# A two-layer sequence mixer: root-mean-square norms by a power on GpSimd, and a rebuilt first stage

## The chip, the core and the metric

The kernel runs on one core of a Trainium2 chip. The metric is the device time of one execution in microseconds (us). TensorE (PE) multiplies matrices, VectorE (DVE) and ScalarE (ACT) do elementwise work, GpSimd (POOL) does a few transfers, a broadcast over partitions and some elementwise work, and SyncE's queue (SP) issues nearly all transfers from memory.

## The reference, cut to what matters

```
def _rmsnorm(x, g):
    y = x * lax.rsqrt(jnp.mean(x * x, axis=-1, keepdims=True) + EPS)
    return y * g

shift, scale, gate = split(silu(c) @ mod_w[layer] + mod_b[layer], 3)
h = _rmsnorm(x, norm_g) * (1 + scale) + shift
# layer 0: u, g = split(h @ rg_w_in); conv over 4 steps; gated linear recurrence; out projection
# layer 1: k, v from their own norm and modulation of x; q, g = split(h @ att_w_in); causal attention; out projection
x = x + gate * y            # after each layer
return _rmsnorm(x, final_norm_g)
```

x is 256 x 1024 in float32, and every weight is 1024 wide. Four norms are taken, two of them of the same x after layer 0.

## The kernel before, in words

x is held as two tiles of 128 rows (s = 0, 1) by 1024. All weights come in blocks of 512 KB from one packed array, in the order of the table `ORDER`, into a ring of 11 buffers (`NRAW`). A product in near float32 is made of three passes: each operand is split into a rounded high part (suffix `_hi`) and the rest (`_lo`), and `mm3` or `gemm_m` adds hi*hi, hi*lo and lo*hi in PSUM.

The program isn't issued as it is written. Each call is recorded by `_Recorder` (line 409 of the profile is the recorder's call, so most rows carry L409; L169 is `Plan.copy` and its kin, which may go to ACT or DVE). `Plan.order` then simulates the engines with fixed costs and writes an order of instructions for each engine; 80 random changes of the urgencies are tried, and the best order is kept. Every engine then takes its instructions strictly in that order. `warm` adds matmuls on a tile of ones that nothing reads ("fillers"); the planner puts them where it sees TensorE idle.

The stages, in the order of time:

1. **First stage.** c, mod_b, norm_g and x are loaded. `rms` squares each row half on ACT with a running sum, takes the root on ACT, and on DVE a reciprocal and one Newton step; `norm_T` scales x by it, and TensorE transposes it (`tp_a`) into xnT. The modulation of the first two groups of 128 columns comes from `mod_one` (32 small matmuls `gvm0s`, then `mc_m0s`), later ones from `mod_pair` or `mod_sum`. `mod_apply` makes h0, split in hi and lo, and `u_rows(k)` (24 matmuls each) and `pair_T` (`ga`) multiply it by the input weights.
2. **Gates and recurrence.** Matmuls `pa` and `px` of the convolved u, then a long row of ACT functions and DVE scans, and the out projection `r_wo`.
3. **Norm b.** x1 = x + gate * y by `resid`; the gate row is gathered by four DMAs on GpSimd's queue (`row_g`) and spread over all partitions by GpSimd's `partition_broadcast` (`gate_g`). Then `rms`, `norm_T`, and the v, k, g and q products, one long run of matmuls.
4. **Attention**, head by head, mixed with the first half of the out projection `r_wp`.
5. **The end.** `fin` runs after each piece of `r_wp`: x2 = x1 + gate * y, `rms` of x2 in two or three parts, times `final_norm_g` (`fgB`), times the root's inverse, and the transfer out. For s = 0 the product with fgB is GpSimd's (two instructions, `ot`); for s = 1 it is DVE's, in place in x2.

The lines that matter most, of `rms`:

```
A.activation(sq, row, AF.Square, accum_out=ss)
A.activation(v, ss, AF.Sqrt, bias=bias, scale=1.0 / D)
V.reciprocal(y, v)
V.scalar_tensor_tensor(t, y, nv, y, ALU.mult, ALU.mult)
V.scalar_tensor_tensor(y, t, 1.5, y, ALU.add, ALU.mult)
```

Of the kernel before, what the change touches and what calls it, by code (L numbers as in the profile page):

```python
# [18 lines left out]
P = 128  # L19
# [7 lines left out]
NRAW = 11  # L27
NSPL = 4
NWARM = 16
NWARM2 = 4  # L30
SUM0 = 3
# [4 lines left out]
    s0 wu0 s1 wu1 wga0 m01 wu2 wu3 m02 wga1 wu4 wu5 m03 wga2 wu6 wu7 wga3 wgc0 gax0 gax2 gax3 g0-0  # L36
    gax1 wgc1 g0-1 wo0 mk0 mk1 wo1 mk4 mk2 mk3 mk5 wv0 mk7 mk6 wv1 wv2 wv3 m10 wka0 wka1 wv4 wv5
    wka2 m12 wv6 m11 wv7 m13 m15 wka3 m14 wkb0 m16 m17 wkb1 wgb0 wgb1 wqa0 wgb2 wgb3 wqa1 wgb4 wgb5
    wqa2 wgb6 wgb7 wqa3 wqb0 wqb1 g1-0 wp0 wp1 g1-1
"""  # L40

# [6 lines left out]
def blocks():  # L48
# [14 lines left out]
    for b in ORDER.split():  # L63
        nm, i = b[:-1], int(b[-1])
        if nm == "s":
            for x, c0 in (("h", 0), ("c", D)):
                want(f"m0{x}0_{i}", (KT, P), ("mod_w", 0, 0, D, c0 + i * P, P))
        elif nm == "m0" and i >= SUM0:
# [31 lines left out]


BLOCKS = blocks()


# [15 lines left out]
class Plan:  # L120
# [165 lines left out]

    def _forward(self, urge):
# [12 lines left out]
        while len(seq) < n:  # L300
# [52 lines left out]
        return max(fin), start, eng, sorted(range(n), key=lambda i: (start[i], i))  # L353

# [7 lines left out]
    def order(self):  # L362
# [15 lines left out]
        rnd = random.Random(self.SEED)  # L378
        for _ in range(self.ROUNDS):
            part, far = rnd.choice((0.003, 0.01, 0.05, 0.3)), rnd.choice((500, 3000, 10000))  # L380
            other = [u + rnd.gauss(0, far) if rnd.random() < part else u for u in urge]
            got = self._forward(other)
            if got[0] <= best[0]:
                best, urge = got, other
# [8 lines left out]
    ROUNDS, SEED = 80, 4  # L393
# [35 lines left out]
def kernel(ctx: ExitStack, tc: tile.TileContext, x, c, mod_b, norm_g, rg_conv_w, rg_conv_b,  # L429
                       rg_b_a, rg_b_x, rg_lambda, kv_norm_g, kv_mod_b, final_norm_g, pack, out):  # L430
# [16 lines left out]
    x, c, out = x[0], c[0], out[0]  # L447
# [13 lines left out]
    def split_into(raw, hi, lo):  # L461
        plan.copy(hi, raw)
        V.tensor_sub(lo, raw, hi.bitcast(F32))


    def wsplit(name):
        while len(halves) <= windex[name]:
# [5 lines left out]
            split_into(t, hi, lo)  # L473
# [86 lines left out]
    th = const.tile([KT, P], F32, name="cth")  # L560
    A.activation(th, c8, AF.Tanh, scale=0.5)
    V.scalar_tensor_tensor(c8, th, 1.0, c8, ALU.add, ALU.mult)
    pt = bank("pt_c")
    PE.transpose(pt[:, 0:KT], c8, ident[0:KT, 0:KT])
    csB = const.tile([P, KT, 32], F32, name="csB")
    V.tensor_scalar(csB, pt[:, 0:KT].unsqueeze(2).broadcast_to([P, KT, 32]), 0.5, None, ALU.mult)
    csT = const.tile([P, KT], F32, name="csT")
    V.tensor_scalar(csT, pt[:, 0:KT], 0.5, None, ALU.mult)
# [3 lines left out]


    def rms(nm, parts, early=None):
        bias, nbias = eps, neps
        for i, row in enumerate(parts):
            w = row.shape[-1]
            sq = tmp.tile([P, w], F32, tag="xn" if w > 512 else "tg", name=f"sq_{nm}{i}")
            if early is not None and i == 0:
                A.activation(sq[0:early.shape[0], 0:1], early, AF.Sqrt, scale=0.0)  # L580
            ss = small.tile([P, 1], F32, tag="ss", name=f"ss_{nm}{i}", bufs=4)
            A.activation(sq, row, AF.Square, accum_out=ss)
            if i < len(parts) - 1:
                b = small.tile([P, 2], F32, tag="rb", name=f"rb_{nm}{i}", bufs=4)
                V.tensor_scalar(b[:, 0:1], ss, 1.0 / D, bias, ALU.mult, ALU.add)
                V.tensor_scalar(b[:, 1:2], ss, -0.5 / D, nbias, ALU.mult, ALU.add)
                bias, nbias = b[:, 0:1], b[:, 1:2]
# [11 lines left out]
    def norm_T(row, rstd, xnT, s, nm):  # L599
        xn = tmp.tile([P, D], F32, tag="xn", name="xn_" + nm, bufs=2)  # L600
        plan.scale(xn, row, rstd)
        for q in range(2):
            ps = pbank(f"tp_{nm}{q}")
            for k in range(4):
                PE.transpose(ps[:, k * P:(k + 1) * P], xn[:, (4 * q + k) * P:(4 * q + k + 1) * P], ident)
            plan.copy(xnT[:, 4 * q:4 * q + 4, s * P:(s + 1) * P], ps.rearrange("p (k n) -> p k n", n=P))

# [179 lines left out]
    for k in range(2):  # L787
        mod_apply("m0", k, 1, m0s[k], xnT, h0_h, h0_l)
        u_rows(k)
# [353 lines left out]
```

## Time and profile before

| | us |
|---|---|
| median of 3 runs | 257.39 (257.09 to 258.31) |
| profiled execution, its time | 257.7 |
| its span in the trace | 255.7 |
| TensorE busy | 242.2 |
| VectorE busy | 208.8 |
| ScalarE busy | 161.2 |
| GpSimd busy | 18.3 |

The span is what the trace covers; 2.0 us of the profiled execution's time lie around it. Busy times are sums of rows of one engine. The busy time of TensorE is partly modelled, so that the starts of matmuls tell more than their lengths. Idle time of an engine is put down to what released it; "issue" means that nothing in the profile explains it.

### The profile page before, as it was taken

The page shows a single profiled execution, that of the slowest core. Times are in us where ns is not written, and L with a number is a line of the kernel's source. Part 1 is how long each engine was busy: PE and PEld are TensorE (multiplying, and loading weights), DVE is VectorE, ACT ScalarE, POOL GpSimd, SP SyncE. Part 2 cuts the span into 40 slices and gives each one's busy share as a digit, 9 for nine tenths or more (in the row PEclk, how much of TensorE's full clock was granted, in tenths as well). Part 3 has the DMA queues.
Part 4 walks back from the last instruction along what each step waited for, and adds up shares of the span by engine and source line. Part 5 has one row for each costly group of instructions (what it writes and reads, how often), then busy time and mean ns, then how long its engine had stood idle before and what let it go on. Part 6 is the DMA issues. An engine that isn't in the chain of part 4 may idle for free.

```text
span 255.7 us, 4865 instructions
## 1 busy us (share of the span) xinstructions
PE 242.2 (95%) x1823; PEld 215.7 (84%) x1823; DVE 208.8 (82%) x378; ACT 161.2 (63%) x288; POOL 18.3 (7%) x31
## 2 busy tenths in 40 slices
PE   8899999999999996997999999999999999999970
PEld 7697799999897874865898898999999998889870
DVE  2773799899969999999898999973766789798483
ACT  7662755595799995079943385863537365786242
POOL 8100000000000033000000000010000000005030
PEclk9999999999999999999999999999999999999996
DMA  6999999992697879999999999986897520000003
GB/s 214 410 417 420 413 420 417 420 415 91 238 352 314 309 270 360 419 396 383 420 316 378 395 393 415 416 299 261 253 354 292 173 82 3 1 0 3 1 17 147
DMA packets 20695, 72.24 MB, mean 283 GB/s; under 512 B 2728, under 2 KB 3008, under 8 KB 20672
## 3 DMA queue, kind: packets, MB, share of 16 engines
q1 hardware_dynamic: 19840, 71.15, 71.9%
q0 software_dynamic: 688, 0.59, 0.9%
q8 instruction: 14, 0.23, 0.4%
q10 hardware_dynamic: 144, 0.20, 0.2%
q14 instruction: 9, 0.07, 0.1%
HBM read 70.87 MB, written 1.05 MB: 281 GB/s over the span
## 4 chain that ended last, share of the span: by engine, by line
PE 77%; ACT 12%; DVE 7%; issue 2%; DVEq 0%; ACTq 0%
PE u L409 9%; PE g L409 9%; PE v L409 9%; PE r_wp L409 6%; PE ga L409 5%; PE pj_wkb L409 5%; PE pj_wqb L409 5%; PE q L409 5%; PE k L409 4%; PE r_wo L409 3%; DVE x L409 3%; PE sc L409 3%; ACT L409 3%; PE warm L409 2%; PE pj_wgc L409 2%
## 5 line engine op out<-in xcount | busy, mean ns | idle before, releaser
L409 ACT ACT_TABLE_LOAD x14 | 18.0, 1283 | 1.0 <-PEq L1126 0.7
L409 PE MATMUL u<-h_lo,wu_hi 128*128 128x256 f32 x64 | 18.1, 285 | 0.0
L409 PE MATMUL u<-h_hi,wu_lo 128*128 128x256 f32 x64 | 18.1, 284 | 0.0
L409 PE MATMUL g<-h_hi,wgb_hi 128*128 128x256 f32 x64 | 18.0, 283 | 0.0
L409 PE MATMUL g<-h_lo,wgb_hi 128*128 128x256 f32 x64 | 18.0, 283 | 0.0
L409 PE MATMUL u<-h_hi,wu_hi 128*128 128x256 f32 x64 | 17.8, 288 | 0.0
L409 PE MATMUL g<-h_hi,wgb_lo 128*128 128x256 f32 x64 | 17.8, 283 | 0.0
L409 DVE SCALAR_TENSOR_TENSOR maccg<-g,csT,maccg 128x1024 f32<-128x1024 f32 x12 | 15.3, 1278 | 1.3 <-DMA g<-in_pack_dram 1.3
L409 POOL DMA_DIRECT2D row_g<-gsg x8 | 4.6, 582 | 142.1 <-issue 142.1
L409 PE MATMUL r_wp<-wp_hi,o_hi 128*128 128x512 f32 (+1 forms) x40 | 14.6, 364 | 0.0
L409 PE MATMUL r_wp<-wp_lo,o_hi 128*128 128x512 f32 (+1 forms) x40 | 14.2, 354 | 0.0
L409 PE MATMUL r_wo<-wo_hi,y_hi 128*128 128x512 f32 x32 | 12.4, 397 | 1.6 <-ACT y_hi L169 1.6
L409 PE MATMUL r_wp<-wp_hi,o_lo 128*128 128x512 f32 (+1 forms) x40 | 13.8, 350 | 0.0
L409 PE MATMUL v<-wv_hi,hk_hi 128*128 128x512 f32 x32 | 12.3, 394 | 1.3 <-ACT hk_hi L169 1.3
L409 PE MATMUL r_wo<-wo_hi,y_lo 128*128 128x512 f32 x32 | 12.3, 394 | 0.4 <-DVE y_lo L409 0.4
L409 DVE TENSOR_TENSOR wgb_lo<-wgb,wgb_hi 128x1024 fp32r<-128x1024 f32 x8 | 9.8, 1222 | 3.5 <-ACT wgb_hi L169 3.5
L409 PEld LDWEIGHTS u<-h_lo,wu_hi 128*128 128x128 f32 x64 | 12.2, 191 | 0.4 <-issue 0.4
L409 PEld LDWEIGHTS u<-h_hi,wu_lo 128*128 128x128 f32 x64 | 12.2, 191 | 0.4 <-issue 0.4
L409 PE MATMUL v<-wv_lo,hk_hi 128*128 128x512 f32 x32 | 12.5, 391 | 0.0
L169 ACT CAST wgb_hi<-wgb 128x1024 fp32r<-128x1024 f32 x8 | 8.4, 1048 | 6.3 <-PE g L409 3.7
L409 PE MATMUL r_wo<-wo_lo,y_hi 128*128 128x512 f32 x32 | 12.4, 397 | 0.0
L409 PEld LDWEIGHTS g<-h_hi,wgb_hi 128*128 128x128 f32 x64 | 12.3, 192 | 0.0
(306 smaller groups left out, 868.6 us busy)
## 6 DMA issues: line engine op xcount, KB each, us to landing
g<-in_pack_dram SPq DMA_DIRECT2D x16, 512.0 KB, 5.0
wu<-in_pack_dram SPq DMA_DIRECT2D x8, 512.0 KB, 10.0
wo<-in_pack_dram SPq DMA_DIRECT2D x8, 512.0 KB, 6.5
mkh<-in_pack_dram SPq DMA_DIRECT2D x8, 512.0 KB, 6.3
mkc<-in_pack_dram SPq DMA_DIRECT2D x8, 512.0 KB, 6.9
wv<-in_pack_dram SPq DMA_DIRECT2D x8, 512.0 KB, 7.3
m1h<-in_pack_dram SPq DMA_DIRECT2D x8, 512.0 KB, 5.2
m1c<-in_pack_dram SPq DMA_DIRECT2D x8, 512.0 KB, 5.3
```

The costliest lines, as they stand in the source:

```text
L169: self.record(eng, fn, args, kw, lambda f=f, args=args, kw=kw: f(*args, **kw))
L409: self.plan.record(self.name, fn, args, kw, lambda: f(*args, **kw))
```

## The change

**Norms.** `rms` squares with a scale of D^-0.5, adds the partial sums and EPS, and takes one power of -0.5 by `G.tensor_tensor(y, v, mhalf, ALU.pow)` on GpSimd. The partial sums of a row in several parts are added on GpSimd too, the last one on DVE. Root, reciprocal and Newton step go, and with them three loads of ACT function tables in the order of ACT (14 before, 11 now).

**The end.** For s = 1 the product with fgB goes to a buffer of its own (`ot`) instead of in place, and so no longer waits for the square; for s = 0 `rms` is recorded behind GpSimd's products.

**First stage.** All small vectors come as one transposed array (`vecs`, one DMA) instead of several and three transposes on TensorE. x has one DMA and one square for each s. The first group of 128 columns has its modulation from `mod_first`: 16 matmuls with the weight block as the stationary operand and one column of c, c's scale part first. h0 of that group is made straight from the transposes in PSUM, and its 24 matmuls go pass by pass. Groups 1 to 3 use `mod_one`, and only 4 and 5 `mod_pair`. The order of the blocks follows. Fillers: 28 and 4 instead of 16 and 4.

**Planner.** The latency of a transfer depends on its time (`_far`); nine fixed changes of the urgencies (`KEEP`) replace the 80 random ones; the ring has 12 buffers.

```diff
-NRAW = 11
+NRAW = 12
-NWARM = 16
+NWARM = 28
...
-    def rms(nm, parts, early=None):
-        bias, nbias = eps, neps
+    def rms(nm, parts, spare=None):
+        bias = EPS
...
-            A.activation(sq, row, AF.Square, accum_out=ss)
+            A.activation(sq, row, AF.Square, scale=D ** -0.5, accum_out=ss)
             if i < len(parts) - 1:
-                b = small.tile([P, 2], F32, tag="rb", name=f"rb_{nm}{i}", bufs=4)
-                V.tensor_scalar(b[:, 0:1], ss, 1.0 / D, bias, ALU.mult, ALU.add)
-                V.tensor_scalar(b[:, 1:2], ss, -0.5 / D, nbias, ALU.mult, ALU.add)
+                b = small.tile([P, 1], F32, tag="rb", name=f"rb_{nm}{i}", bufs=4)
+                G.tensor_scalar(b, ss, bias, None, ALU.add)
...
-        A.activation(v, ss, AF.Sqrt, bias=bias, scale=1.0 / D)
-        nv = small.tile([P, 1], F32, tag="rn", name="rn_" + nm)
-        V.tensor_scalar(nv, ss, -0.5 / D, nbias, ALU.mult, ALU.add)
+        V.tensor_scalar(v, ss, bias, None, ALU.add)
         y = small.tile([P, 1], F32, tag="ry", name="ry_" + nm)
-        V.reciprocal(y, v)
-        t = small.tile([P, 1], F32, tag="rt", name="rt_" + nm)
-        V.scalar_tensor_tensor(t, y, nv, y, ALU.mult, ALU.mult)
-        V.scalar_tensor_tensor(y, t, 1.5, y, ALU.add, ALU.mult)
+        G.tensor_tensor(y, v, mhalf, ALU.pow)
         return y
...
+    def mod_first(nm, m, gain, bias, both, new):
+        cp = new(f"mc_{nm}{m}")
+        for w in (1, 0):
+            t = got[f"{nm}{'hc'[w]}{m // 2}_{m % 2}"]
+            for kt in range(KT):
+                PE.matmul(cp[:, w:w + 1], t[:, kt], csT[:, kt:kt + 1], start=(w == 1 and kt == 0),
+                          stop=(w == 0 and kt == KT - 1), skip_group_check=True)
...
-        rstd = rms(f"f{s}", [x2[:, s, q] for q in parts], None if s else sms[-1][:, 0:1])
         ot = tmp.tile([P, D], F32, tag="xn", name=f"ot{s}")
         rows_ = out[s * P:(s + 1) * P]
         if s == 0:
             for q in parts:
                 G.tensor_mul(ot[:, q], x2[:, s, q], fgB[:, q])
+        rstd = rms(f"f{s}", [x2[:, s, q] for q in parts])
+        if s == 0:
+            for q in parts:
                 plan.scale(ot[:, q], ot[:, q], rstd)
             SP.dma_start(rows_, ot)
         else:
-            plan.after = (last,)
             for q in parts:
-                V.tensor_mul(x2[:, s, q], x2[:, s, q], fgB[:, q])
-            plan.after = ()
-            A.activation(ot[:, 0:CUT], x2[:, s, 0:CUT], AF.Identity, scale=rstd)
-            V.tensor_scalar(ot[:, CUT:], x2[:, s, CUT:], rstd, None, ALU.mult)
+                V.tensor_mul(ot[:, q], x2[:, s, q], fgB[:, q])
+            A.activation(ot[:, 0:CUT], ot[:, 0:CUT], AF.Identity, scale=rstd)
+            V.tensor_scalar(ot[:, CUT:], ot[:, CUT:], rstd, None, ALU.mult)
```

GpSimd, the second half of its list, before. An "ISA" row without a tile is, in the built program, a load of a set of GpSimd code, named by a number: set 0 has the elementwise operations, set 1 the broadcast. An "ISA" row with `gate_g` is the broadcast.

```order
L409 DMA row_g_381<-gsg_380 1x16x16 x4
L409 ISA
L409 ISA gate_g_382<-row_g_381 128x1024
L409 DMA fgB<-in_final_norm_g_dram 128x1024
L409 DMA row_g_585<-gsg_584 1x16x16 x4
L409 ISA gate_g_586<-row_g_585 128x1024
L409 ISA
L409 TENSOR_TENSOR ot_632<-x_601,fgB 128x512 x2
```

And now, from the load of set 0 behind the first broadcast on:

```order
L432 ISA
L432 TENSOR_SCALAR rb_b_383<-ss_b_382 128x1
L432 TENSOR_TENSOR ry_b_387<-rv_b_386,mhalf 128x1
L432 TENSOR_SCALAR rb_b_393<-ss_b_392 128x1
L432 TENSOR_TENSOR ry_b_397<-rv_b_396,mhalf 128x1
L432 DMA fgB<-in_final_norm_g_dram 128x1024
L432 DMA row_g_568<-gsg_567 1x16x16 x4
L432 ISA
L432 ISA gate_g_569<-row_g_568 128x1024
L432 ISA
L432 TENSOR_TENSOR ot_606<-x_584,fgB 128x512 x2
L432 TENSOR_SCALAR rb_f_609<-ss_f_608 128x1
```

Set 0 is now loaded before norm b, so set 1 has to be loaded again between the second `row_g` and the second broadcast, and set 0 again behind it. `rb_f`, and behind it the power `ry_f`, stand behind both products `ot`.

DVE, at the end, now. `rv_f` needs GpSimd's `rb_f`; x_584 is x2, `ot_614` the rows s = 1, `ot_606` the rows s = 0:

```order
L432 TENSOR_TENSOR x_584<-r_wp_587,gate_g_569 128x512
L432 TENSOR_SCALAR rv_f_612<-ss_f_611,rb_f_609 128x1
L432 TENSOR_TENSOR x_584<-x_584,x_349 128x512
L185 TENSOR_SCALAR ot_606<-ot_606,ry_f_613 128x512
L432 TENSOR_TENSOR x_584<-r_wp_588,gate_g_569 128x256
L432 TENSOR_TENSOR ot_614<-x_584,fgB 128x512
L432 TENSOR_TENSOR x_584<-x_584,x_349 128x256
L432 TENSOR_TENSOR x_584<-r_wp_589,gate_g_569 128x256
L432 TENSOR_TENSOR ot_614<-x_584,fgB 128x256
L432 TENSOR_TENSOR x_584<-x_584,x_349 128x256
L432 TENSOR_TENSOR ot_614<-x_584,fgB 128x256
L432 TENSOR_SCALAR rv_f_623<-ss_f_622,rb_f_620 128x1
```

Before, no instruction of DVE in this place waited for GpSimd except the scaling of the rows s = 0.

TensorE, from its start to the first product of the first stage, now (`warm` and `ga<-ones` are fillers):

```order
L432 MATMUL warm<-ones 128x128 x20
L432 MATMUL tp_a_232<-ident,xn_a_231 128x128 x4
L432 MATMUL tp_a_233<-ident,xn_a_231 128x128 x4
L432 MATMUL warm<-ones 128x128 x2
L432 MATMUL tp_a_238<-ident,xn_a_237 128x128 x4
L432 MATMUL tp_a_239<-ident,xn_a_237 128x128 x4
L432 MATMUL mc_m_241<-csT,m0c_0_82 128x1 x8
L432 MATMUL mc_m_241<-csT,m0h_0_83 128x1 x8
L432 MATMUL warm<-ones 128x128 x6
L432 MATMUL ga_250<-ones 128x128 x4
L432 MATMUL u_245<-h_hi,wu_hi 128x256 x2
```

Before, 16 fillers stood ahead of the transposes and 4 between them, none directly ahead of the first product. Every float32 matmul of this list is two rows in a trace (the 16 fillers `warm` of before are 32 rows), a transpose one.

## Rows read from the trace of the kernel before

**Rows 1.** The page: busy us of each engine, share of the span, rows
```profile
PE 242.2 (95%) x1823; PEld 215.7 (84%) x1823; DVE 208.8 (82%) x378; ACT 161.2 (63%) x288; POOL 18.3 (7%) x31
```
**Rows 2.** Stretches: length; busy us (rows) of PE, PEld, DVE, ACT, POOL; clock, DMA share, GB/s
```profile
95.00:100.00 5.00, 3.44 (x38) 1.85 (x31) 4.97 (x8) 3.35 (x5) 0.91 (x1) 1.00 0.95 332
...
115.00:120.00 5.00, 3.59 (x25) 2.49 (x18) 4.71 (x10) 4.71 (x12) 0.00 (x0) 1.00 1.00 376
```
**Rows 3.** The chain that ended last, first stage: start us, us, what
```profile
1.05 2.92 PE warm L409 x12
...
4.17 3.12 PE warm L409 x18
...
10.77 0.80 PE tp_a L409 x6
...
12.69 0.67 PE ga L409 x6
13.36 1.01 PE gvm0s L409 x32
14.37 0.90 PE u L409 x6
...
20.52 2.31 PE gvm L409 x32
...
23.74 0.34 PE mc_m L409 x4
...
61.46 1.30 PE px L409 x6
```
**Rows 4.** Timeline, TensorE's weight loads: start us, us, engine line operation out<-in xcount
```profile
12.42 0.75 PEld L409 LDWEIGHTS ga<-ones 128*128 128x128 f32 x6
...
23.46 0.54 PEld L409 LDWEIGHTS mc_m<-sel,partm 128*128 128x128 f32 x4
```
**Rows 5.** Timeline, GpSimd; in brackets the idle time ahead and what ended it
```profile
1.74 0.29 POOL L409 TENSOR_SCALAR_AFFINE_SELECT maskf<-maskf 128x128 f32<-128x128 f32 x1
...
99.09 2.20 POOL L409 PARTITION_BROADCAST gate_g<-row_g  x1 [6.64 <-issue]
...
229.89 2.15 POOL L409 DMA_DIRECT2D row_g<-gsg  x4 [59.91 <-issue]
233.27 1.50 POOL L409 PARTITION_BROADCAST gate_g<-row_g  x1 [1.23 <-DMA row_g<-gsg]
242.40 1.28 POOL L409 TENSOR_TENSOR ot<-x,fgB 128x512 f32<-128x512 f32 x1 [7.63 <-PE r_wp L409]
244.30 1.30 POOL L409 TENSOR_TENSOR ot<-x,fgB 128x512 f32<-128x512 f32 x1 [0.63 <-DVE x L409]
```
**Rows 6.** The tile row_g from 88 to 98 us: time to landing of its transfers
```profile
DMA to landing us min/median/max: 2.8/3.8/4.2
```
**Rows 7.** The chain that ended last, norm b
```profile
113.83 1.15 ACT xn_b L169
...
116.79 0.94 ACT wv_hi L169
...
117.98 11.22 PE v L409 x48
```
**Rows 8.** Timeline, DVE and ACT at the end
```profile
240.81 0.69 DVE L409 TENSOR_TENSOR x<-x,x 128x512 f32<-128x512 f32 x1
...
248.76 0.42 DVE L409 TENSOR_TENSOR x<-x,x 128x256 f32<-128x256 f32 x1
249.09 0.69 DVE L409 TENSOR_TENSOR x<-x,fgB 128x512 f32<-128x512 f32 x1
249.27 0.42 ACT L409 ACTIVATE sq_f<-x 128x256 f32<-128x256 f32 x1 [0.67 <-DVE x L409]
...
249.69 0.21 DVE L409 TENSOR_SCALAR rb_f<-ss_f,rb_f 128x1 f32<-128x1 f32 x1
...
251.36 0.55 DVE L409 TENSOR_SCALAR ot<-x,ry_f 128x640 f32<-128x640 f32 x1 [0.22 <-DVE ry_f L409]
```

More of the change, by code (lines that the diff above doesn't have):

```diff
@@ L65, in blocks @@
         if nm == "s":
[L66 to L68 removed]
+            for x, c0 in (("c", D), ("h", 0)):
+                want(f"m0{x}{i // 2}_{i % 2}", (KT, P), ("mod_w", 0, 0, D, c0 + i * P, P))
+        elif b == "m03":
             for q in range(4):
@@ L102, with columns @@
 BLOCKS = blocks()
+VECTORS = ("c", "mod_b", "norm_g", "rg_conv_w", "rg_conv_b", "rg_b_a", "rg_b_x", "rg_lambda", "kv_norm_g", "kv_mod_b")
+NV = 160
+def columns(inputs):
+    import numpy as np
+    return np.concatenate([inputs[n].reshape(-1, P) for n in VECTORS]).astype(np.float32).T
 def packed(inputs):
@@ L284, in _tails, with _far @@
         return tail
+    @staticmethod
+    def _far(done):
+        return max(950, 2200 - 0.069 * (done - 6200)) if done > 6000 else 950
     def _forward(self, urge):
@@ L353, in _forward, with _shake @@
         return max(fin), start, eng, sorted(range(n), key=lambda i: (start[i], i))
+    @staticmethod
+    def _shake(urge, k):
+        rnd = random.Random(k)
+        part, far = rnd.choice((0.001, 0.003, 0.01, 0.05, 0.3)), rnd.choice((500, 3000, 10000))
+        return [u + rnd.gauss(0, far) if rnd.random() < part else u for u in urge]
     def _on(self, i, e):
@@ L376, in order @@
         best = self._forward(urge)
[L378 to L384, printed above, removed]
+        if KEEP:
+            for k in KEEP:
+                urge = self._shake(urge, k)
+            best = self._forward(urge)
         self.span, self.start, eng, seq = best
@@ L785, in u_rows @@
         gemm_T(ub, wh, wl, h0_h, h0_l, kt)
-    for k in range(2):
+    t4 = m0s[0]
+    hr = tmp.tile([P, S], F32, tag="hr", name="hr_first", bufs=3)
+    for s in range(ST):
+        sl = slice(s * P, (s + 1) * P)
+        A.activation(h0_h[:, 0, sl], tps[s][0][:, 0:P], AF.Identity, bias=t4[:, 0, 0:1], scale=t4[:, 0, 1:2])
+        V.tensor_scalar(hr[:, sl], tps[s][0][:, 0:P], t4[:, 0, 1:2], t4[:, 0, 0:1], ALU.mult, ALU.add)
+    V.tensor_sub(h0_l[:, 0], hr, h0_h[:, 0].bitcast(F32))
+    first = len(plan.ops) - 1
+    m0s.append(mod_one("m0", 1, *args0))
+    wh, wl = wsplit("wu_0", (first,))
+    for i, (w, h) in enumerate(((wh, h0_h), (wh, h0_l), (wl, h0_h))):
+        for m in range(KT):
+            PE.matmul(ub[m // 2][:, (m % 2) * S:(m % 2 + 1) * S], w[:, m * P:(m + 1) * P], h[:, 0],
+                      start=(i == 0 and m % 2 == 0), stop=False, skip_group_check=True)
+    started = len(plan.ops) - 1
+    for k in range(1, 4):
         mod_apply("m0", k, 1, m0s[k], xnT, h0_h, h0_l)
+        if k < 3:
+            m0s.append(mod_one("m0", k + 1, *args0))
+        else:
+            nxt = mod_pair("m0", 2, *args0)
         u_rows(k)
-    nxt = mod_pair("m0", 1, *args0)
-    pair_T(gb, "wga", h0_h, h0_l, 0)
-    pt = pbank("pt_b")
-    PE.transpose(pt[:, 0:88], pb, ident[0:88, 0:88])
-    pbT = const.tile([P, 88], F32, name="pbT")
-    V.tensor_copy(pbT, pt[:, 0:88])
+        if k % 2:
+            pair_T(gb, "wga", h0_h, h0_l, k // 2)
+    pbT = vT[:, KT + 64:]
     cwT = pbT[:, 0:32].rearrange("p (j k) -> p j k", j=4)
@@ L805 @@
     argsk = (kvnT, pair_bias("mk", kvbT))
+    plan.after = (started,)
     nl = const.tile([P, KT], F32, name="nl")
     V.tensor_scalar(nl, lamT, -1.0, None, ALU.mult)
+    plan.after = ()
     na = const.tile([P, KT], F32, name="na")
@@ L830 @@
     V.tensor_scalar(n8, sp, -8.0, None, ALU.mult)
-    for i in range(1, 4):
+    for i in range(2, 4):
         mod_apply("m0", 2 * i, 2, nxt, xnT, h0_h, h0_l)
         if i < 3:
-            nxt = (mod_pair if i + 1 < SUM0 else mod_sum)("m0", i + 1, *args0)
+            nxt = mod_sum("m0", i + 1, *args0)
         for kt in (2 * i, 2 * i + 1):
@@ L1087, in fin @@
         r2(s, sl, b)
-        last = len(plan.ops) - 1
         if sl.stop < D:
@@ L1130 @@
     inputs["pack"] = packed(inputs)
+    inputs["vecs"] = columns(inputs)
     for name in _INS:
```

116 lines of the change are left out of this document (56 added, 60 removed).

## The prediction

> **What bounds the kernel now.** I read the engines' shares first: TensorE is busy 95% of the span, VectorE 82%, ScalarE 63%, GpSimd 7% [rows 1]. The reader should see that TensorE leaves 13.5 us of 255.7, so work on another engine counts only where TensorE waits for it: at the start, around norm b and at the end. In the stretches, TensorE is idle 1.56 us between 95 and 100 and 1.41 us between 115 and 120 [rows 2]: about 3.0 us is all that norm b can give back. Then I read the chain of waits. In the first stage it runs on TensorE from the first filler to the gates: the first product u starts at 14.37 and the first gate matmul px at 61.46, with matmuls all the way [rows 3]; nothing there waits for a weight. Whatever delays the first u, or adds matmuls before px, therefore delays px. Last I read GpSimd's own timeline, because the change puts it on the path of every norm [rows 5].
>
> **GpSimd's code loads, the main term.** Ahead of the first broadcast stands a load of code set 1. The broadcast starts at 99.09, after 6.64 us that nothing in the profile explains [rows 5]; the queue was thus free of row_g's transfers at 92.45, and they land at most 4.2 us after issue [rows 6], so by 96.7. Ahead of the second broadcast there is no load, and it starts 1.23 us after the queue is free, on landing. Behind it stands a load of set 0, and the first product ot starts 7.63 us after the broadcast's end; the second ot is released by VectorE's x [rows 5], while x for the first was done at 241.50 (240.81 + 0.69 [rows 8]), 0.9 us before its start. I read 6.64 us for a load of set 1 and 7.63 us for set 0, each starting when the engine reaches it. The lower bound is set by the alternative that part of each gap was other waiting: 99.09 less 96.7, 2.4 us, and 0.9 us.
>
> Before, both long gaps lay where nobody waited. Now set 0 is needed for norm b, so set 1 must come back between row_g and the second broadcast, and set 0 behind it. In the time of the trace before: row_g is done on the queue at 232.04 (229.89 + 2.15) [rows 5]; four more matmuls of about 0.23 us stand behind its source in TensorE's order, so 0.9 us earlier, 231.14. Plus 6.64 gives 237.8. The broadcast that followed a load took 2.20 us, the other 1.50 [rows 5]; I take 2.20, so the gate is there at 240.0, just in time for the first residual product. Plus 7.63 gives 247.6 for the first ot, which started at 242.40. Two ot of 1.28 and 1.30, and then rb_f: 250.2 + 0.3, so VectorE can start rv_f at 250.5. **That wait blocks VectorE**: queued behind rv_f are the residual add of 512 columns, the scaling of rows s = 0, and five more products and adds ahead of the last add. By starts of rows, 512 columns take 0.60 us (249.09 to 249.69) and 256 columns 0.33 (248.76 to 249.09) [rows 8]. rv_f 0.13, add 0.60, scaling 0.39, 256, 512, 256, 256 and 256 wide 0.33 + 0.60 + 3 x 0.36, and the last add 0.42 in full: 3.5 us. The square of the last 256 columns runs from 249.27 until VectorE reads its sum at 249.69, 0.42, and with hops 0.6; rv_f 0.3, the power 0.3, a hop 0.1. So the last scaling starts 4.9 to 5.0 us after 250.5, at 255.5; it started at 251.36 [rows 8]. **The end: +4.1 us.** Without the loads, rb_f would still stand behind the second ot (245.6), and the last scaling would start at 250.95: the Newton step and root that go are worth 0.4 us there.
>
> The power itself has no row. Bounds: above, 1.28 us, a GpSimd instruction of 512 columns; below, nothing much, 0.1 us. Nearest is the affine_select of 128 columns, 0.29 us [rows 5]; I take 0.3. It is once on the path at the end and once in norm b, so the upper bound costs 1 us at each.
>
> The Trainium skill, GPSIMD Engine Reference, Instruction dispatch, says that the first call to freshly loaded code pays a load of about 6 us (5.95 measured) that has no row of its own. The gaps here, 6.64 and 7.63 us, agree with it in kind and are longer. By the page's figure for both loads the end would be 2.4 us shorter, +1.7 instead of +4.1; the sum goes by the rows.
>
> **First stage.** Fillers of before: 12 rows in 2.92 us, then 18 in 3.12 [rows 3]. Now 40 rows stand first. The same 30 end at 7.09, and ten more at the rate of late fillers (six in 0.67, 0.112 each [rows 3]) at 8.2. The vectors for the transposes are ready before that, since x lands as before. Then 8 transposes at 0.133 (six in 0.80 [rows 3]), 4 filler rows, 8 transposes: 10.8. Then mc_m, 16 matmuls, 32 rows that each load 128 x 128 float32 weights for one column. Bounds per row: 0.085 (four in 0.34 on the chain [rows 3]) and 0.135 (four loads in 0.54 [rows 4]). I take 0.112, the longest run of such loads (six in 0.75 or 0.67 [rows 3, 4]): 3.6 us, 14.4. Then 20 filler rows that stand ahead of the first u, 2.2 us: **16.6 instead of 14.37, +2.2** (1.4 to 2.9 over the bounds). Behind it, three single modulations of 1.01 and a pair replace two pairs of 2.31 [rows 3]: 3.03 - 2.31, **+0.7**. The three transposes that go are shorter than 0.3 us each and lay among fillers; the table loads and tiny VectorE steps that go were covered by TensorE's own rows there. Fewer transfers ahead of x save issue time on SP, but x's place in the queue is second, as before.
>
> **Norm b.** The chain goes from xn_b (113.83) over two transposes and a cast of wv (0.94 us) to the first v at 117.98 [rows 7]. In the new order xn_b can't start earlier: VectorE's 1.2 us low part of wv now stands ahead of rv_b, in place of the Newton steps. But the cast moves ahead of xn_b and the third copy behind the first hk. That is 0.94 + 0.58, less some 0.3 for the next groups, **-1.2** (0 to -3.0, all the idle time there [rows 2]). Set 0 is back at 101.29 + 7.63 = 108.9, as the first partial sum comes; if the load were longer than that, norm b would lose the surplus. The gates do the same ACT work in another order: nothing. Attention loses one table load of ACT under matmuls of r_wp: nothing. The middle from 118 to 228 is TensorE's, with the same matmuls: nothing; the twelfth buffer lets transfers run ahead that nobody waits for.
>
> **Sum.** 257.7 (span 255.7 and 2.0 around it) + 2.2 + 0.7 - 1.2 + 4.1 = 263.5 for that execution; it lies 0.3 above the median of 257.39, so **263.2 us**.
>
> **Rivals.**
>
> A. *The loads are cheap where it counts, and the kernel isn't slower by a measurable amount.* Place: the two loads around the second broadcast. It decides at a sum of 9.7 us for both (then the first ot starts by 243.0 and the second is bound by its operand as before); the rows give 14.3 as read, 3.3 at the lowest. For it: a gap may hold other waiting, and the 0.9 us lateness of ot is the only delay seen against an operand. Against it: both gaps are of one size. Time: 257.4 + 2.9 - 1.2 - 0.4 = 258.7, within 0.5% or at its edge.
>
> B. *The first stage doesn't lengthen.* It decides at 0.055 us per row of mc_m and filler (10.8 + 52 rows = 13.65, which also pays for the extra modulation). For it: the ends of matmuls are modelled, and one column is little work. Against it: no row with 128 x 128 float32 weights is under 0.085. Time: 257.4 - 1.2 + 4.1 = 260.3.
>
> A and B together: 257.4 - 1.2 - 0.4 = 255.8, faster.
>
> **How the numbers follow.** About 0.5% (1.3 us) is what a measurement of this kernel can tell from no change. My forecast has 0.52, and its own range is 259.9 (first stage +2.1, norm b -3.0, broadcast 1.50) to 267.1 (first stage +3.6, norm b 0, power at its upper bound). B has 0.18, slower as well. A has 0.15, counted as no change. A with B has 0.10, faster. 0.05 is left for what I don't see, split 0.02, 0.01, 0.02. So slower 0.72, same 0.16, faster 0.12. The range takes in A, B and most of the forecast, 257.0 to 265.5; A with B and the forecast's worst end are left out.
>
> **What would show it.** GpSimd idle some 6 us ahead of the second broadcast and 7 behind it, VectorE idle 3 us or more ahead of rv_f, and the last scaling 5 us behind rv_f: the main term right. A first ot within 0.1 us of its operand: A. The first u near 16.6 and px near 64.4 on the new time: the first stage right; u before 14: B. Wrong altogether if the first v comes more than 3 us earlier than px's shift explains, or if the power takes over 1.3 us.

## The result, and the profile after

The changed kernel takes 269.64 us (median of 4 runs, 267.89 to 269.93) against 257.38 (4 runs) before: **1.0448 times as long** (95% interval 1.0422 to 1.0474), 12.3 us more. Slower was forecast, 263.2 us, with a range up to 265.5: the direction was right, the size outside the range. The profiled execution took 269.93 us, its span is 267.6 (before 255.7).

The page's busy shares, as in [rows 1], say little: TensorE is busy 7.4 us longer, with 51 rows more of 1823.

```profile
PE 249.6 (93%) x1874; PEld 225.9 (84%) x1874; DVE 205.7 (77%) x344; ACT 155.6 (58%) x281; POOL 20.7 (8%) x35
```

The way to read the loss is by places that both kernels have, as starts in TensorE's timeline: first u, first gate matmul (pa or px), first v, end of the last r_wp (modelled, as all ends of matmuls), end of the span.

| us | before | after | difference |
|---|---|---|---|
| start to first u | 14.30 | 19.05 | +4.75 |
| to the first gate matmul | 47.00 | 47.72 | +0.72 |
| to the first v | 56.68 | 59.90 | +3.22 |
| to the end of the last r_wp | 129.96 | 130.69 | +0.73 |
| to the end | 7.76 | 10.24 | +2.48 |
| sum | 255.70 | 267.60 | +11.90 |

**First stage.** The chain that ended last, against [rows 3] (start, us, what):

```profile
9.20 1.05 PE tp_a L432 x8
10.25 4.67 PE mc_m L432 x32
14.92 2.77 PE warm L432 x12
17.69 1.63 PE ga L432 x8
19.32 0.23 PE u L432 x2
```

Up to 10.25 it runs as forecast (10.8). Then the fillers, 0.112 us a row before, take 0.23 (2.77 / 12). The stretches say why (columns: length; busy us and rows of PE, PEld, DVE, ACT, POOL; granted clock; DMA share; GB/s):

```profile
11.00:12.00 1.00, 1.00 (x11) 1.00 (x11) 0.00 (x0) 0.92 (x1) 0.00 (x0) 1.00 0.98 401
12.00:13.00 1.00, 1.00 (x8) 1.00 (x7) 0.00 (x0) 0.00 (x0) 0.00 (x0) 0.64 1.06 434
13.00:14.00 1.00, 1.00 (x6) 1.00 (x6) 0.00 (x0) 0.00 (x0) 0.00 (x0) 0.50 1.00 410
```

The granted clock falls from 1.00 to 0.50, from 2.4 to 1.2 GHz, in the middle of mc_m, the matmuls of one column, and stays there under the fillers until 19. TensorE's busy column is full all the while: a busy share of 100% didn't tell that the clock was about to fall.

**Norm b.** GpSimd's timeline, with the idle time ahead in brackets, against [rows 5]:

```profile
103.65 1.81 POOL L432 PARTITION_BROADCAST gate_g<-row_g  x1 [6.59 <-issue]
116.71 0.25 POOL L432 TENSOR_SCALAR rb_b<-ss_b 128x1 f32<-128x1 f32 x1 [11.26 <-ACT sq_b L432]
117.29 1.51 POOL L432 TENSOR_TENSOR ry_b<-rv_b,mhalf 128x1 f32<-128x1 f32 x1 [0.33 <-DVE rv_b L432]
118.89 0.22 POOL L432 TENSOR_SCALAR rb_b<-ss_b 128x1 f32<-128x1 f32 x1
122.40 0.95 POOL L432 TENSOR_TENSOR ry_b<-rv_b,mhalf 128x1 f32<-128x1 f32 x1 [3.29 <-DVE rv_b L432]
```

and VectorE's in the same place, against [rows 7]:

```profile
114.20 0.69 DVE L432 TENSOR_TENSOR x<-x,xr 128x512 f32<-128x512 f32 x1
117.00 0.21 DVE L432 TENSOR_SCALAR rv_b<-ss_b,rb_b 128x1 f32<-128x1 f32 x1 [2.10 <-POOL rb_b L432]
117.13 1.22 DVE L432 TENSOR_TENSOR wv_lo<-wv,wv_hi 128x1024 fp32r<-128x1024 f32 x1
118.26 0.68 DVE L432 TENSOR_TENSOR x<-r_wo,gate_g 128x512 f32<-128x512 f32 x1
118.98 0.69 DVE L432 TENSOR_TENSOR x<-x,xr 128x512 f32<-128x512 f32 x1
120.97 1.22 DVE L432 TENSOR_TENSOR wv_lo<-wv,wv_hi 128x1024 fp32r<-128x1024 f32 x1 [1.30 <-ACT wv_hi L185]
122.11 0.21 DVE L432 TENSOR_SCALAR rv_b<-ss_b,rb_b 128x1 f32<-128x1 f32 x1
```

Two things stand here. VectorE waits 2.10 us for rb_b, whose own operand, the first partial sum, was complete at 113.73 (ScalarE's first square of x, read out). And the last product and add of x, on which the second norm depends, stand behind that wait and behind a low part of wv (1.22), and the second rv_b behind another low part that waits for its cast. The first v comes at 126.67; before, at 117.98. What TensorE waits for in between are the second transposes, of the rows s = 1 (before, and below it after):

```profile
115.51 1.14 PE L409 MATMUL tp_b<-ident,xn_b 128*128 128x128 f32 x8
```

```profile
125.06 1.97 PE L432 MATMUL tp_b<-ident,xn_b 128*128 128x128 f32 x8 [3.93 <-ACT x1T L185]
```

They come behind 3.93 us of idle time, and take 1.97 us instead of 1.14, as the granted clock is at 0.50 from 124.92 to 128.33.

**The end**, against [rows 5] and [rows 8]:

```profile
246.39 1.30 POOL L432 PARTITION_BROADCAST gate_g<-row_g  x1 [5.83 <-DVE wp_lo L432]
254.45 2.54 POOL L432 TENSOR_TENSOR ot<-x,fgB 128x512 f32<-128x512 f32 x2 [6.75 <-issue]
257.08 0.26 POOL L432 TENSOR_SCALAR rb_f<-ss_f 128x1 f32<-128x1 f32 x1
257.68 0.97 POOL L432 TENSOR_TENSOR ry_f<-rv_f,mhalf 128x1 f32<-128x1 f32 x1 [0.33 <-DVE rv_f L432]
```

```profile
257.38 0.21 DVE L432 TENSOR_SCALAR rv_f<-ss_f,rb_f 128x1 f32<-128x1 f32 x1 [2.16 <-POOL rb_f L432]
...
263.05 0.55 DVE L432 TENSOR_SCALAR ot<-ot,ry_f 128x640 f32<-128x640 f32 x1 [0.68 <-POOL ry_f L432]
```

Both loads lie where they were forecast. VectorE stands idle at rv_f too, but for 2.16 us, where the forecast's sign was 3 us or more; the last scaling comes 5.7 us behind it.

### The profile page after: what moved, and what is told of

It reads as the page before. It is cut to its first block, busy times and chain, and to the rows that moved or that the text cites. A ratio compares the mean times of both kernels' runs of the same rounds, so it can differ in the third digit from the quotient of the medians.

```text
span 267.6 us, 4911 instructions
## 1 busy us (share of the span) xinstructions
PE 249.6 (93%) x1874; PEld 225.9 (84%) x1874; DVE 205.7 (77%) x344; ACT 155.6 (58%) x281; POOL 20.7 (8%) x35
## 4 chain that ended last, share of the span: by engine, by line
PE 79%; ACT 6%; DVE 5%; issue 3%; POOL 2%; DMA 2%; POOLq 0%; DVEq 0%; ACTq 0%
PE u L432 9%; PE g L432 9%; PE v L432 8%; PE r_wp L432 6%; PE ga L432 5%; PE pj_wkb L432 4%; PE pj_wqb L432 4%; PE q L432 4%; PE k L432 4%; PE r_wo L432 4%; PE warm L432 4%; PE sc L432 2%; DVE x L432 2%; PE pj_wgc L432 2%; PE oT L432 2%
## 5 line engine op out<-in xcount | busy, mean ns | idle before, releaser
L432 PE MATMUL u<-h_hi,wu_hi 128*128 128x256 f32 x64 | 17.2, 292 | 0.0
L432 PE MATMUL u<-h_lo,wu_hi 128*128 128x256 f32 x64 | 17.1, 287 | 0.0
L432 PE MATMUL u<-h_hi,wu_lo 128*128 128x256 f32 x64 | 16.9, 284 | 0.0
L432 PE MATMUL r_wo<-wo_hi,y_hi 128*128 128x512 f32 x32 | 12.6, 400 | 1.5 <-ACT y_hi L185 1.5
L432 PE MATMUL v<-wv_hi,hk_hi 128*128 128x512 f32 x32 | 13.1, 410 | 0.0
L432 PEld LDWEIGHTS u<-h_hi,wu_hi 128*128 128x128 f32 x64 | 11.6, 192 | 1.0 <-issue 1.0
L432 PEld LDWEIGHTS g<-h_hi,wgb_hi 128*128 128x128 f32 x64 | 12.3, 192 | 0.0
L432 PEld LDWEIGHTS g<-h_lo,wgb_hi 128*128 128x128 f32 x64 | 12.3, 192 | 0.0
L432 PEld LDWEIGHTS g<-h_hi,wgb_lo 128*128 128x128 f32 x64 | 12.3, 192 | 0.0
```

Source lines behind the costliest of these rows:

```text
L432: self.plan.record(self.name, fn, args, kw, lambda: f(*args, **kw))
```

## The experiments

In all of them the planner records and orders every instruction as in the kernel that the experiment is made from (the one before for e7, else the changed one); only what an instruction does, or its place, is changed afterwards. So no experiment has a new plan. Times are medians, ratios are to the kernel before, run again beside each group of experiments (its medians there: 257.36 to 258.08). The diffs are cut to what they change. The places come from one profiled execution of each, which can lie some 2 us off the median (e3's took 266.74 us, e10's 262.57), and a place that an experiment doesn't touch can move by 0.8 (the first u of e2); "low clock" tells whether TensorE's granted clock fell to 0.50 there, ahead of or just behind the first u, and around norm b.

| | time, ratio [95%] | first u | to gates | to v | to last r_wp | to end | low clock |
|---|---|---|---|---|---|---|---|
| before | 257.38 | 14.30 | 47.00 | 56.68 | 129.96 | 7.76 | no, no |
| after | 269.64, 1.0448 | 19.05 | 47.72 | 59.90 | 130.69 | 10.24 | yes, yes |
| e1 | 267.25, 1.0364 [1.0318, 1.0410] | 17.52 | 48.48 | 58.59 | 131.69 | 9.12 | yes, yes |
| e2 | 265.51, 1.0325 [1.0291, 1.0359] | 19.85 | 47.70 | 57.88 | 131.41 | 8.06 | yes, yes |
| e3 | 268.78, 1.0438 [1.0387, 1.0488] | 16.20 | 47.72 | 59.23 | 130.43 | 11.02 | no, yes |
| e4 | 267.10, 1.0389 [1.0355, 1.0423] | 16.57 | 47.71 | 58.02 | 131.48 | 10.82 | no, yes |
| e5 | 265.25, 1.0282 [1.0245, 1.0319] | 17.57 | 47.72 | 58.59 | 131.87 | 9.15 | no, yes |
| e6 | 265.78, 1.0317 [1.0266, 1.0368] | 16.50 | 47.70 | 59.51 | 131.86 | 10.33 | no, yes |
| e7 | 259.93, 1.0093 [1.0061, 1.0125] | 14.43 | 47.27 | 56.69 | 129.89 | 10.82 | no, no |
| e8 | 264.45, 1.0265 [1.0232, 1.0299] | 17.41 | 47.72 | 56.20 | 131.94 | 9.13 | no, no |
| e9 | 266.61, 1.0333 [1.0288, 1.0378] | 16.66 | 47.70 | 56.67 | 133.85 | 10.22 | no, yes |
| e10 | 264.30, 1.0248 [1.0213, 1.0282] | 16.49 | 47.71 | 56.18 | 132.40 | 8.02 | no, no |
| e11 | 267.24, 1.0349 [1.0308, 1.0390] | 17.68 | 49.25 | 56.28 | 133.94 | 8.05 | yes, yes |
| e12 | 260.62, 1.0127 [1.0087, 1.0167] | 15.54 | 47.74 | 56.18 | 131.07 | 8.07 | no, no |

### e1 to e3: whose work is it, GpSimd's or the order's?

```diff
-                G.tensor_scalar(b, ss, bias, None, ALU.add)
+                V.tensor_scalar(b, ss, bias, None, ALU.add)
...
-        G.tensor_tensor(y, v, mhalf, ALU.pow)
+        V.tensor_scalar(y.bitcast(I32), v.bitcast(I32), -0.5, 1597463007.0, ALU.mult, ALU.add)
+        V.tensor_scalar(nv, v, -0.5, None, ALU.mult)
+        for _ in range(2):
+            V.scalar_tensor_tensor(t, y, nv, y, ALU.mult, ALU.mult)
+            V.scalar_tensor_tensor(y, t, 1.5, y, ALU.add, ALU.mult)
```

e1 does this in all norms, e2 in norm b alone, e3 in norm f alone.

> Every sum rb and every power ry of the norms moves from GpSimd to VectorE, in the changed kernel's order of all other instructions; the power becomes a start value from the bits of v and two Newton steps, six tiny VectorE instructions. GpSimd then has no elementwise work between the first broadcast and the products ot, so one load of set 1 and one of set 0 go. Theory (of the 11.9 us lost, norm b's 3.6 and the end's 2.7 belong to GpSimd's loads and to VectorE and ScalarE waiting in order behind its tiny steps, the front's 5.5 do not): norm b comes back by 3.6 to 4.8, the end by 2.5 to 3.1, the front by nothing; time 261.7 to 263.5, first u still at 19.3. Rival (the new order of norm b and of the end is what costs, whichever engine takes the power): less than 2 us come back, 267.6 or more.

> Only norm b's sums and powers move to VectorE; norm f's stay on GpSimd. No set 0 is needed between the two broadcasts, so both extra loads go with it. Theory (loads): norm b gives back 3.6 to 4.8, and at the end the second broadcast starts 1.2 us behind row_g, the first ot about 3.5 us earlier against the last matmuls, so the end gives back 2 to 2.7 as well: 262.0 to 264.0. Rival (tiny steps: at the end it is rb_f and the power themselves and VectorE's wait for them that cost, not the loads): the end keeps its 2.7, time 264.8 to 266.0.

> Only norm f's sums and powers move to VectorE; norm b's stay on GpSimd, so all loads stay. Theory (loads): the products ot still end 257.0 us after the start, and the scaling of the rows s = 0 waits for them in VectorE's order instead of rv_f, so only rb_f's 0.26 and some 0.5 to 0.7 of the power come back: 268.4 to 269.1. Rival (tiny steps): the end gives back 2 to 2.7, 266.9 to 267.6.

e1 came out at 267.25, by its number nearly the rival's: the stretch to v gives back only 1.3 of 3.2, and the longer chains on VectorE in norm a and at the end take from the gain. e2's time, 265.51, missed its range as well and lies in the rival's: norm b gives back 2.0 instead of 3.6 to 4.8. But the place that was to decide is the end, and it goes against the rival: with norm f still on GpSimd, the last r_wp to the end takes 8.06, 0.3 more than before. Its rows:

```profile
241.30 1.29 POOL L434 PARTITION_BROADCAST gate_g<-row_g  x1 [1.25 <-DMA row_g<-gsg]
250.21 1.29 POOL L434 TENSOR_TENSOR ot<-x,fgB 128x512 f32<-128x512 f32 x1 [7.61 <-DVE x L434]
```

Set 1 was still there for the second broadcast (1.25 behind row_g, as in [rows 5]). In e3, where the loads stay and norm f is VectorE's, the end takes 11.02: taking rb_f and the power away from GpSimd gives nothing back there, and 268.78 is the theory's. By itself e3 couldn't decide, as VectorE's own chain for norm f costs about 1 us (the end takes 9.12 in e1 and 8.06 in e2, both without the loads). With e2 it does: **the end's loss is the loads'**, not the tiny steps'. Of norm b, more than half stays in e1.

### e4: the clock

```diff
-                PE.matmul(cp[:, w:w + 1], t[:, kt], csT[:, kt:kt + 1], ...)
+                PE.matmul(cp[:, w * 128:w * 128 + 128], t[:, kt], csT[:, kt:kt + 1].broadcast_to([P, 128]), ...)
```

> The 16 matmuls mc_m of the first stage multiply 128 equal columns of c instead of one; only one column of each result is read, everything else is as in the changed kernel. Theory (the granted clock fell to 0.50 at 12.3 us because one-column matmuls give TensorE next to no work, and half of mc_m and the 20 filler rows behind it ran at the lower level): the clock stays at 1.00, 32 rows of mc_m take 3.6 us instead of 4.67, the 20 filler rows 2.2 instead of 4.4, first u at 16.0 to 16.8 instead of 19.3, time 266.4 to 267.2. Rival (the clock falls for another reason, such as the transfers that run then): clock 0.50 between 12.5 and 19 as before, time 269 to 270.

267.10 us, as the theory has it. The chain of e4, and below it that of e3, which has the one-column mc_m and happened to keep the clock:

```profile
10.56 3.59 PE mc_m L735 x32
...
16.57 0.50 PE u L433 x2
```

```profile
10.29 3.48 PE mc_m L434 x32
...
16.20 0.51 PE u L434 x2
```

128 columns cost 0.1 us more than one for all 32 rows (3.59 and 3.48). Over the profiled executions, the clock fell in mc_m or the fillers behind it in three of four with one column (after, e1, e2, not e3), and ahead of the first u in none of the eight with 128 columns (e4 to e6, e8 to e12). That the narrow matmuls are the cause is shown as far as such a count goes; the rival of e4, the transfers, is ruled out, as e4 moves as much at that time (406 to 424 GB/s between 10 and 16 us, with the clock at 1.00). When it falls differs: some 2 us after mc_m's start in the changed kernel, 4.7 in e1, whose first u is at 17.52 instead of the 19.3 expected. e3's profiled execution doesn't stand for its median: the three others took 268.3 to 270.0 us at a mean granted clock of 0.96 to 0.97, against 0.98.

### e7: the loads alone, in the kernel before

```diff
         G.partition_broadcast(gb, row)
+        if l == 0:
+            G.tensor_scalar(dummy, neps, 1.0, None, ALU.mult)
```

> The kernel before, in its own order, with one GpSimd instruction on 128x1 that nobody reads behind the first broadcast: set 0 is loaded there, and set 1 and set 0 have to be loaded once more around the second broadcast. Theory (a load of set 1 costs 5.8 to 6.6 us, of set 0 6.8 to 7.6): second broadcast at 237.0 to 238.0 instead of 233.27, first ot at 245.5 to 247.5 instead of 242.40, VectorE's scaling of the rows s = 0 waits 1 to 3 us for it; norm b as before; time 258.5 to 260.5. Rival A (the loads are hidden behind row_g and the last matmuls): 257.0 to 257.8.

259.93, 2.6 us more (1.0093, 1.0061 to 1.0125). GpSimd's rows:

```profile
98.93 1.65 POOL L409 PARTITION_BROADCAST gate_g<-row_g  x1 [6.05 <-issue]
111.54 0.26 POOL L753 TENSOR_SCALAR dummy<-neps 128x1 f32<-128x1 f32 x1 [10.96 <-issue]
...
238.37 2.37 POOL L409 PARTITION_BROADCAST gate_g<-row_g  x1 [5.97 <-issue]
248.29 2.48 POOL L409 TENSOR_TENSOR ot<-x,fgB 128x512 f32<-128x512 f32 x2 [7.56 <-PE r_wp L409]
```

Nearly the whole difference is at the end (10.82 instead of 7.76), where VectorE waits 1.88 us for ot. (The second broadcast and the first ot lie somewhat behind their expected ranges; the profiled execution, of 261.07 us, is the longest of the five.) One more thing stands in the second row: the dummy waits for no operand, and still it starts 10.96 us behind the broadcast. That is the load of set 0 in this stretch, and it explains norm b's first wait: in the changed kernel rb_b starts 11.26 behind the broadcast, in e3, e4 and e9 10.5 to 10.7, each time 1.7 to 3.0 us after its operand.

### e5, e6, e8, e9: the order of norm b

e5 is e1 and e4 together. e8 and e9 move four or five instructions, by place in the issue order:

```diff
+        move(at("vector", "wv_0_lo"), at("gpsimd", "ry_b1"))
+        move(at("scalar", "wv_1_hi"), at("scalar", "sq_b11"))
+        move(at("vector", "wv_1_lo"), at("vector", "hrmk"))
+        move(at("vector", "wv_2_hi"), at("vector", "wv_1_lo"))
```

This is e8, on e5's kernel, where the norms are VectorE's (`ry_b1` names their place). e9, on e4's, has GpSimd's norms, and puts the last two and wv_2_lo behind the first `hk_lo`. e6, on e4's, moves x's last product and the squares as well.

> The norms on VectorE and the 128 equal columns of mc_m together, in the changed kernel's order. Theory (the three losses lie one behind the other, each in its own place): first u at 16.2 to 16.8, norm b still 1.4 to 2.2 us longer than before from its first row sum gvmk to the first v (9.0 to 9.8 against 7.58), because the order of VectorE and ScalarE there stays; time 264.0 to 265.4. Rival (what is won in the front is only waited for later, as the weights of the middle set the pace): 266.5 or more.

> Norms on VectorE, wide mc_m, and norm b's order changed as far as it makes sense without GpSimd: low part of wv_0 behind the second power, cast of wv_1 behind the last square, low part of wv_1 and cast of wv_2 behind the first modulation. Theory (with the order mended norm b costs no more than before): from the first gvmk to v 6.5 to 7.8, end 0.3 to 1.3 longer than before, front 2.2 + 0.7 longer; time 260.8 to 263.0. Rival (norm b is bound by something that stays): gvmk to v 9 or more, time 264 or more.

> Wide mc_m, norms on GpSimd as in the changed kernel, and of norm b only the order mended: low part of wv_0 behind the second power, ScalarE's cast of wv_1 behind the last square, low parts of wv_1 and wv_2 and the cast of wv_2 behind the first low part of hk. Theory (of norm b's 3.2 us the order has about 2, GpSimd's late first sum and its powers about 1): from the first gate matmul to the first v 56.2 to 57.4 (before 56.7, with the wide mc_m alone 58.0), time 264.6 to 266.2. Rival (VectorE stands behind rb_b whatever the order): 57.8 or more, time 266.6 or more.

> The wide mc_m, norms on GpSimd, and in norm b four instructions in another place of their engine's order: VectorE's low part of wv_0 behind the second power instead of ahead of the last x product, the low part of wv_1 and the cast of wv_2 behind the first modulation, ScalarE's cast of wv_1 ahead of the last square instead of behind it, and the last square ahead of the first xn_b. Theory (the new order costs most of norm b's loss, GpSimd's late first step and powers the smaller part): from the first gvmk to v 6.6 to 8.0 instead of 9.1, time 264.6 to 266.2. Rival (GpSimd alone costs norm b): 8.8 or more, time 266.5 or more.

e5's time is in its range, and the losses nearly add: e1 gave back 2.4, e4 2.5, both together 4.4. Its first u isn't: 17.57 instead of 16.2 to 16.8, as norm a's chain is longer on VectorE. From gates to v, e8 takes 56.20 against e5's 58.59, and e9 with GpSimd's norms 56.67 against e4's 58.02: the order is worth 1.35 to 2.4 there, and with it norm b is no longer than before. Some 0.8 of the 2.4 is the clock, which fell in e5 ahead of the second transposes (1.97 us for 8 rows, 1.15 in e8). The wait ahead of these shows the order most directly: 3.42 us in e5 and 1.36 in e8, 3.56 in e4 and 2.22 in e9. VectorE in e8:

```profile
113.35 0.21 DVE L447 TENSOR_SCALAR rv_b<-ss_b,rb_b 128x1 f32<-128x1 f32 x1
...
114.69 0.68 DVE L447 TENSOR_TENSOR x<-r_wo,gate_g 128x512 f32<-128x512 f32 x1
115.41 0.69 DVE L447 TENSOR_TENSOR x<-x,xr 128x512 f32<-128x512 f32 x1
...
118.22 1.22 DVE L447 TENSOR_TENSOR wv_lo<-wv,wv_hi 128x1024 fp32r<-128x1024 f32 x1
```

But the totals missed (264.45 and 266.61): I had put the moved low parts ahead of the low parts of hk, and v then waited for those (e8's front, at 17.41, is also 0.9 longer than forecast, with norm a on VectorE):

```profile
124.19 0.73 PE L447 MATMUL v<-wv_hi,hk_lo 128*128 128x512 f32 x2 [1.65 <-DVE hk_lo L447]
```

In e9 that wait is 2.02 and the clock falls just behind it (125.64, 126.16). e6 can't be read for norm b: x's last product was issued ahead of the last two r_wo products, which are therefore left out of that quarter of x, and TensorE waited 3.01 us for x. That its time lies in the theory's range is an accident.

### e10 to e12: putting the places together

e10 is e4, norm b on VectorE (e2), and e9's order. e11 adds, in the first stage, mc_m's first half ahead of the transposes and its second half between them, with ten fillers fewer.

> Wide mc_m, norm b on VectorE (norms a and f stay on GpSimd), norm b's order mended as in the run beside it. Theory (what is left is the first stage's work and 0.3 at the end): first u 16.2 to 16.8, first gate matmul 47.7 later, first v 56.0 to 56.6 later, last r_wp 130.0 to 131.0 later, then 8.0 to 8.4 to the end: 260.4 to 262.4. Rival (what norm b gains is waited for by the products behind it, 131.5 or more from the first v to the last r_wp): 262.6 or more.

> The same, and in the first stage the scale half of mc_m ahead of the first transposes, the shift half between the two groups of transposes, 16 + 2 + 4 filler matmuls instead of 20 + 2 + 10. Theory (behind mc_m a chain of five small steps on VectorE and ScalarE stood alone ahead of the first u; the transposes can cover it): first u at 14.2 to 15.2, time 258.4 to 260.6, still not below the kernel before, as three single modulations and a pair stay (0.7). Rival (the weight block for mc_m lands too late for that): first u 16 or more, time 260.6 or more.

> All repairs at once, and the two of the last runs that came out wrong mended: in the first stage ScalarE takes the first modulation ahead of the copies of the second transposes, so that mc_m between the transposes can help; behind norm b the low parts of wv_1, wv_2 and the casts stand between the low parts of hk, not ahead of them. Theory (the loss is the sum of places that have been found, and nothing else): first u 14.8 to 15.6, first gate matmul 47.7 later, from there to the last r_wp 186.5 to 187.7 (before 186.6), end 8.0 to 8.4: time 259.0 to 261.0. Rival (a loss that has not been found, in the middle): from the first gate matmul to the last r_wp 188.5 or more, time 261.5 or more.

e10 missed by v's wait again (2.14 us, for the second low part of hk; 132.40 from v to the last r_wp, the rival's). e11 came out at the rival's number, but not by its reason, a late weight block: it missed because ScalarE had the copies of the second transposes and a cast ahead of the first modulation; TensorE, with fewer fillers, stood idle for 2.78 us ahead of the first u, and the clock fell behind it. Both are faults of my orders, of the same kind as the planner's in norm b. e12 mends them, in e11's kernel:

```diff
-        move(at("vector", "wv_2_hi"), at("vector", "wv_1_lo"))
-        move(at("vector", "wv_2_lo"), at("vector", "wv_2_hi"))
+        move(at("vector", "wv_2_hi"), at("vector", "x1_", 7))
+        move(at("vector", "wv_2_lo"), at("vector", "hk_lo", 2))
+        move(at("vector", "wv_3_hi"), at("vector", "wv_2_lo"))
+        move(at("vector", "macm1h"), at("vector", "wv_3_hi"))
+        move(third, at("scalar", "h0_hi", 1))
+        move(fourth, third)
```

(`third` and `fourth` are the copies of the second transposes, `x1_`, 7 is x's last add.) **260.62 us**, every place within its expected range. Of the changed kernel's 12.3 us, 8 to 9 are back (8.3 by the ratios, 9.0 by the medians). What is left against before, by places: first u +1.24, modulations +0.74, gates to v -0.50, v to r_wp +1.11 (0.75 of it a wait for a low part of wv), end +0.31. No version here beat the kernel before.

## Why the prediction was wrong, step by step

The forecast's terms add up to 5.8 us, and 11.9 were measured. First u came 2.55 later than its term says, norm b cost 4.4 more, the middle, put at nothing, 0.7, and the end 1.6 less. The forecast's own worst case (267.1) is passed too: the granted clock stands in none of its terms and in no rival.

**First stage: the term was mis-sized, by the clock.** The forecast took mc_m and the 20 filler rows at 0.112 us a row, first u at 16.6 instead of 14.37. With the clock at 1.00 the number is right: 16.20 in e3, 16.57 in e4. That is in part luck: a chain of small steps behind mc_m that the forecast didn't name, from `sg2m` to the second `h_hi`, ends at the same time as the fillers, and it is what ended last there:

```profile
15.69 0.47 ACT h_hi L434
```

(e3's chain, ahead of its u; in e4 TensorE waits 0.21 us for it.) The forecast assumed that the clock stays up, as under the fillers of before. It fell; mc_m took 4.67 instead of 3.6 and the fillers 4.40 (2.77 + 1.63) instead of 2.2. That is 2.85 of the loss (19.05 - 16.20). The modulations' +0.7 measured +0.72.

**Norm b: the step failed, by its sign.** It said that "xn_b can't start earlier" and then credited 1.2 us for a cast that moves; +3.2 came to the first v, and +0.7 behind it. Three things were missed. First, I compared what stands ahead of rv_b, not what stands behind it: x's last product behind VectorE's wait and a low part, the last square behind ScalarE's first xn_b and a cast. In order, each of these passes its lateness on. Second, "set 0 is back at 108.9" took a load of 7.63 us from the end; here it takes 10.5 to 11.7, and the forecast itself had said that norm b would lose the surplus. Third, the power takes 1.51 and 0.95 us, not 0.3. By the runs the order has 1.35 to 2.4 of it (e9, e8). Moving norm b to VectorE gave back 1.31 (e1), 0.64 (e5 against e3) and 0.14 (e2 against e4), in pairs with the clock alike ahead of v; that follows VectorE's wait for rb_b, 2.10, 1.46 and 0.83, so GpSimd's share looks to be its lateness, which changes from one execution to the next. The clock has some 0.8 ahead of v (the second transposes at 1.97 instead of 1.14) and, as an estimate, half of the 1.66 us that it stays at 0.50 behind v, which is the 0.7 there. These shares overlap and can't simply be added. The clock fell in each of the six executions (after, e1 to e5) in which TensorE stood idle 3.4 to 3.9 us ahead of the second transposes, and not there in e8, e10 and e12, with 1.36 us.

**The end: right mechanism, over-sized.** +4.1 forecast, +2.48 measured; e2, e3 and e7 show that it is the two loads. The broadcast started 5.83 behind the queue (forecast 6.64) and lasted 1.30 (2.20), and the first ot came 6.75 behind it (7.63): 2.6 us less. The chain behind rv_f was 0.7 longer (5.7 instead of 5.0), with powers of 0.97 and 0.56 where the forecast had 0.3 once. The Trainium skill, GPSIMD Engine Reference, Instruction dispatch, has about 6 us for the first call to freshly loaded code. The loads of set 1 agree, with 5.8 to 7.0 in all runs; those of set 0 are longer (6.7 to 7.6 at the end).

**The rivals.** A (loads cheap) is refuted by e7, and the two gaps around the second broadcast add up to 12.6 us in the changed kernel, where A needed less than 9.7. B (first stage not longer) is refuted by e3 and e4: 16.2 at best, with 0.109 us a row of mc_m (3.48 / 32) where B needed 0.055. The check named in the forecast for "wrong altogether" (the power over 1.3 us) was met, once.

## What to carry to other kernels

An engine that takes its instructions in order turns one late operand into lateness of everything behind it: before moving a tiny step to another engine, list what stands behind the waiting instruction, and put that ahead if it doesn't need the operand. A GpSimd instruction of another kind between two broadcasts costs a load of code each way, 6 to 12 us here, and it must be hidden at both ends. Matmuls of one column kept TensorE's busy share at 100% here and still lost the clock in three of four executions; widening them to 128 columns cost 0.1 us.

## What the runs showed of the hardware

- The load of set 0 took 6.7 to 7.6 us at the end of the kernel and 10.5 to 11.7 after the first broadcast, with (e9) or without (e7) an operand to wait for. In the changed kernel's gap at the end (247.69 to 254.45) nothing is moved, in the one after the first broadcast (105.46 to 116.71) 410 GB/s; that the transfers slow the load wasn't tried.
- The power on 128x1 took 0.57 us twice in norm a, where VectorE had nothing to do, and 1.51 beside VectorE's low part of wv (117.13 to 118.35), 0.95 beside its cast (0.60 and 1.48 in e9, beside a product that reads PSUM and beside a low part). The Trainium skill, SBUF — State Buffer, Who interferes with whom, says that VectorE and GpSimd share a pair of ports: a VectorE instruction with two SBUF inputs contends there with a GpSimd instruction that reads SBUF, and when VectorE is in a mode that takes both ports, whoever issues first has the pair for its whole instruction. The trace agrees with it: beside the low parts and beside the cast, each power ends 0.43 to 0.45 us behind the end of VectorE's instruction. The other way round it shows in e3: two of VectorE's tiny steps took 1.01 and 1.20 us, against 0.22 and 0.16 for the same steps behind them, while GpSimd's ot ran:

```profile
252.32 1.01 DVE L591 SCALAR_TENSOR_TENSOR rt_f<-ry_f,rn_f 128x1 f32<-128x1 f32 x1
253.37 1.20 DVE L592 SCALAR_TENSOR_TENSOR ry_f<-rt_f,ry_f 128x1 f32<-128x1 f32 x1
254.60 0.22 DVE L591 SCALAR_TENSOR_TENSOR rt_f<-ry_f,rn_f 128x1 f32<-128x1 f32 x1
254.85 0.16 DVE L592 SCALAR_TENSOR_TENSOR ry_f<-rt_f,ry_f 128x1 f32<-128x1 f32 x1
```

- The four executions of e3 spread from 266.74 to 270.00 us (the kernel before beside it 257.01 to 257.44), with mean granted clocks from 0.980 to 0.964. Why the clock falls in one execution and not in another stays open.
